# TensorE's order: from edges behind a planner to the program's own text, in a four-branch decoder step

## The chip, the cores and the metric

One core of a Trainium2 chip. The metric is the device time of one execution in microseconds; the median of the runs counts. A core has TensorE (PE in the profile; its weight loads are shown apart as PEld), VectorE (DVE), ScalarE (ACT), GpSimd (POOL) and SyncE (SP), which issues most DMAs. Each engine works through its own instruction queue in order, and waits there for semaphores.

## The reference

One inference step of a two-layer decoder trunk, d_model 1024, for 1024 prompt tokens and 64 sample tokens (8 sequences of 8) with shared weights. Everything is float32.

```
layer 0 (even): proj = rmsnorm(x) @ w_in_even
  branch A: y_a = a_b * short_conv(a_c * a_h) * silu(a_z)
  branch B: r, k, v, w, a from the token-shifted projection
            S = S*decay + (S @ -kk)*(kk*a) + v*k ;  y = S @ r      # a scan over time, 8 heads x 64
            y_b = (groupnorm(y) + bonus) * silu(b_z)
  x += concat(y_a, y_b) @ w_out_even
layer 1 (odd): proj = rmsnorm(x) @ w_in_odd
  branch C: y_c = (causal window means of 2, 4, 8, 16 - p) @ pool_w * scale * silu(c_z)
  branch D: y_d = u * (tril(W) @ layernorm(v) + b) * silu(d_z)
  x += concat(y_c, y_d) @ w_out_odd
y = rmsnorm(x)
```

The final states (convolution, shift, S, pooling) are outputs too.

## The kernel before

The activations lie transposed, features on partitions, tokens along the free axis. The 1088 tokens (64 sample, 1024 prompt) are cut into three blocks b0, b1, b2 of 320, 384 and 384 (`BLK`); b0 holds the sample and two groups of 128 prompt tokens, the others three groups each.

**Dense work.** A projection is a sequence of weight tiles of 128 output columns. `product` computes one tile for one block: for each of eight k-tiles three matmuls (lines 162, 163, 164) of split operands, hi x hi, hi x lo, lo x hi, so 24 matmuls into one PSUM tile ("dn"). Four k-tiles, 12 matmuls, are a half product; `marks` keeps the last instruction of each half. `weight` (from line 138) loads a raw tile in two pieces over SP's queue, casts it on ScalarE (whi, line 145) and subtracts on VectorE (wlo, line 146); each has `WB` = 4 buffers, two to a product. Layer 0 has 33 input tiles per block (13 shifted ones, 4 for the gate b_z, 16 for branch A in `mixer_a`) and 8 output tiles; layer 1 has 20 and 8.

**Branch B** is made of small matmuls. `rwkv_prep` prepares a group: decays and norms (lines 487, 488, 496), key transposes (521), score matrices of two chunks of 64 tokens (555, 64 matmuls), the bonus (577) and value transposes (584). `rwkv_inverse` inverts all triangular score blocks of a block on VectorE, 31 dependent pairs of operations (610, 612), between DMAs to and from DRAM on POOL's queue. `rwkv_merge` joins the halves of an inverse (639, 651). `rwkv_chunk` is the recurrence over chunks, each chunk's state SV coming from the chunk before (761, 770 and 775; then 780; then 786 and 788). `group_norm` and `group_out` (732) finish a group and store it to DRAM (`yr`), from where `out_proj0` loads it. `rwkv_sample` does the eight sample sequences (825, 846, 847, 858, 864, 883); at 858 it needs block 0's inverse. The PSUM tiles "pp" (4 buffers) serve all of these.

**What sets the order.** The program runs under a planner that orders every engine's instructions by priorities and by its own estimate of when inputs are ready; `tc.high_priority()` (also called `urgent`) puts a part ahead. TensorE's dense matmuls are chained by `later()`, an edge that says "not before the last product", and the branch's generators are walked in `recur`, each step with an edge "not before the half product `marks[x]`". These edges only say what a matmul comes after; what it comes before is the planner's choice, one matmul at a time.

**Order of the program.** b0: input tiles, preparation and inverse, `mixer_a`; b1: input tiles, `mixer_a`, then traced behind it, with the priority of `boost`, the recurrence of b0, the sample, and the preparation and inverse of b1; b2 likewise with the recurrence of b1; then output tiles of b0 and b1 with the recurrence of b2; output tiles of b2; layer 1. In layer 1 `pool_in(g)` makes six products, `windows` sums them on VectorE, and `pool_out` (line 1230) multiplies the sums; `layer_norm` (1146, 1166) works on ten token tiles.

Of the kernel before, what the change touches and what calls it, by code (L numbers as in the profile page):

```python
# [18 lines left out]
AT = (10, 10, 0)  # L19
EARLY, RATE, PREP_RATE = 20, 0.7, 0.5  # L20
# [53 lines left out]
def build(nc, tc, a):  # L74
    from contextlib import ExitStack
    ctx = ExitStack()

# [72 lines left out]
    order, marks = {}, []  # L150

    def later():

        return tc.issue_after(order["last"]) if order else ExitStack()

    def product(ps, w, h, c0, n):

        with later():
            for k in range(KT):
                wh, wl = w[k // 4]  # L160
                hh, hl = h[k]
                mm(ps, wh[:, k % 4, :], hh[:, c0:c0 + n], start=k == 0, stop=False)  # L162
                mm(ps, wh[:, k % 4, :], hl[:, c0:c0 + n], start=False, stop=False)  # L163
                i = mm(ps, wl[:, k % 4, :], hh[:, c0:c0 + n], start=False, stop=k == KT - 1)  # L164
                if k in (3, 7):
                    marks.append(getattr(i, "ins", i))
        order["last"] = marks[-1]
# [114 lines left out]
    def rms_token(B):  # L282
        B.ms0 = mk(ev, [128, 4], "rms_m", 2)
        with later():
            token_rstd(B.acc, B.n, B.ms0, pd, "dn")

    def rms_spread(B):
        with later():
            B.rstd = spread_rstd(B.ms0, B.n, ev, pd, "dn")
# [451 lines left out]
    def rwkv_chunk(B, g, c, parts, yps):  # L741
# [23 lines left out]
        first = state.get("y")  # L765
        for e in range(2):
            for p in range(4):
                if p == 0:
                    with (tc.issue_after(first) if first is not None else ExitStack()):
                        i = mm(yps[half[e], cols(p, 256 * c)], AR[half[e], p, c, 1, :], SV[half[e], p, e, :],  # L770
                               start=True, stop=False, skip_group_check=True)
                    first = getattr(i, "ins", i)
        with tc.issue_after(first):
            for p, e in heads[2:]:
                mm(yps[half[e], cols(p, 256 * c)], AR[half[e], p, c, 1, :], SV[half[e], p, e, :],
                   start=False, stop=False, skip_group_check=True)
# [10 lines left out]
        for p, e in heads:  # L787
            i = mm(yps[half[e], cols(p, 256 * c)], GT[:, 2 * p + e, 64:128], UV[:, p, e, :], start=False, stop=True,
                   skip_group_check=True)
        state["y"] = getattr(i, "ins", i)  # L790
# [14 lines left out]
    def rwkv_sample(B, now):  # L805
# [45 lines left out]
        up = pp()  # L851
# [75 lines left out]
    def late_rstd(psp, pname, pb=2):  # L927

        while late:
            B, acc = late.pop()  # L930
            B.ms = mk(cpool, [128, 4], f"ms1_{B.i}")
            with later(), urgent():
                token_rstd(acc, B.n, B.ms, psp, pname, pb)
# [12 lines left out]
    def recur(B, at, nxt=None):  # L946


        done, merged, now = [0], [0], [0]
        start = at  # L950
# [8 lines left out]
        def chain():  # L959
# [3 lines left out]
            for g in range(B.ng):  # L963
# [14 lines left out]
                done[0] += 1  # L978
# [5 lines left out]
        def prep():  # L984
            for q, x in enumerate(nxt.gl):
                while done[0] < min(q + 1, B.ng):
                    yield
                yield from rwkv_prep(nxt, *x)
                yield

        streams = [[at, RATE, merge()], [at, RATE, chain()]]
        if B.i == 0:
            streams.append([at - EARLY, RATE, rwkv_sample(B, now)])
        if nxt is not None:
            rwkv_begin(nxt)
            streams.append([at, PREP_RATE, prep()])
        while streams:
            x = min(streams, key=lambda x: x[0])
            now[0] = x[0] >= start
            with (tc.issue_after(marks[int(x[0])]) if x[0] < len(marks) else ExitStack()):  # L1000
                if next(x[2], 0) is not None:
                    streams.remove(x)
            x[0] += x[1]
        for p in range(4):
            ydr[(B.i, 4 + p)] = B.yr[:, p, :]

    def boost(mark):
        return tc.high_priority(tc.cur_priority - mark)
# [12 lines left out]
    mark = tc.cur_priority  # L1021
# [4 lines left out]
    rms_spread(b1)  # L1026
    mixer_a(b0, hs[0], (3,))
    hs.append(rms_h(b1))
    at = len(marks)
# [11 lines left out]
    at = len(marks)  # L1041
    rwkv_in(b2)
    mixer_a(b2, hs[2], range(4))
    with boost(mark):
        recur(b1, at + AT[1], b2)
        rwkv_inverse(b2)
    at = len(marks)
    out_proj0(b0)
    out_proj0(b1)
    with boost(mark):  # L1050
        recur(b2, at + AT[2])
# [73 lines left out]
    with later(), urgent():  # L1125
        norm1(b2)
# [4 lines left out]
    with tc.issue_after(order["last"]):  # L1131
        mm(ps, ones, ws.rearrange("p g t -> p (g t)"), start=True, stop=True)
# [3 lines left out]
    with tc.issue_after(order["last"]):  # L1136
        mm(ps[:, 0:256], ones[0:64], wss.rearrange("p g t -> p (g t)"), start=True, stop=True)
# [32 lines left out]
    def layer_norm(at):  # L1170
        last = None
        for ti in range(10):
            with tc.issue_after(marks[at + ti]):
                nx = ln_a(ti) if ti < 9 else None
            if last:
                with tc.issue_after(marks[at + ti + 1]):
                    ln_b(*last)
            last = nx
# [45 lines left out]
    def pool_out(g, cz, pl_):  # L1224
        yc = big()
        y1.append(yc)
        for B in Bs:
            ps = mk(pl, [128, 512], "pl", None)[:, :B.n]
            with later():
# [4 lines left out]
    at, last = len(marks), None  # L1234
    for g in range(4):
        cz, ep, es = pool_in(g)
        if g == 0:
            with urgent():
                layer_norm(at)
# [41 lines left out]
    def final_token(B):  # L1281
        B.msf = mk(e1p, [128, 4], "rms_m", 2)
        with later():
            token_rstd(accs[B.i], B.n, B.msf, pl, "pl", PLB)

    def final(B):
        with later():
            r = spread_rstd(B.msf, B.n, hp, pl, "pl", "rx", pb=PLB)
# [92 lines left out]
```

## Time and profile before

| | |
|---|---|
| median of 3 runs | 1141.25 us (1135.46 to 1141.45) |
| the profiled execution: time, span | 1138.0 us, 1136.2 us |
| mean granted TensorE clock | 0.967 |
| TensorE busy, weight loads busy | 1090.4 us (96%), 1003.7 us (88%) |
| VectorE busy | 729.5 us (64%) |
| ScalarE, GpSimd busy | 491.5 us (43%), 164.4 us (14%) |

The span goes from the first to the last instruction. TensorE's busy time is the union of its matmuls' times, whose ends are modelled, so a busy TensorE need not be one that works at its best. [...]

### The profile page before, as it was taken

How to read it: one execution, taken by the hardware profiler on the slowest of the kernel's cores; microseconds unless marked ns; L12 is line 12 of the kernel's file. 1: busy time of each engine (PE TensorE's matmuls, PEld its weight loads, DVE VectorE, ACT ScalarE, POOL GpSimd, SP SyncE). 2: the span in 40 equal slices, each digit the busy share in tenths (PEclk: the TensorE clock that was granted, in tenths of full speed). 3: DMA queues.
4: the chain of work that ended last, by engine and by line, in shares of the span. 5: the costliest groups of instructions: out<-in, count | busy, mean ns of one | idle time of the engine just before them, and what ended most of it. 6: DMA issues, size and time to landing. Idle time of an engine off the chain costs nothing.

```text
span 1136.2 us, 22856 instructions
## 1 busy us (share of the span) xinstructions
PE 1090.4 (96%) x8719; PEld 1003.7 (88%) x8719; DVE 729.5 (64%) x1526; ACT 491.5 (43%) x1017; POOL 164.4 (14%) x282
## 2 busy tenths in 40 slices
PE   7999999999999999999899999999999999999996
PEld 6998999876756899878799889899999999999995
DVE  7878899457632799478797477695373442245456
ACT  6376654365412554666535654464212111133232
POOL 2313343110301212113301011001010100000000
PEclk9999999899966999999999999899999999999998
DMA  8464563554412454535545687775201111112455
GB/s 263 149 212 129 157 206 123 146 157 145 128 58 65 121 189 125 140 104 150 155 152 149 185 242 222 228 254 186 79 21 55 38 48 38 53 41 91 116 154 183
DMA packets 135341, 154.91 MB, mean 136 GB/s; under 512 B 45560, under 2 KB 88696, under 8 KB 135232
## 3 DMA queue, kind: packets, MB, share of 16 engines
q1 hardware_dynamic: 130912, 146.36, 41.8%
q0 software_dynamic: 2256, 5.03, 2.2%
q10 hardware_dynamic: 2064, 2.08, 0.6%
q8 instruction: 68, 1.11, 0.4%
q14 instruction: 41, 0.34, 0.1%
HBM read 127.77 MB, written 25.64 MB: 135 GB/s over the span
## 4 chain that ended last, share of the span: by engine, by line
PE 40%; DVE 5%; DMA 4%; issue 1%; ACT 1%; POOL 1%; SPq 0%; DVEq 0%; ACTq 0%; POOLq 0%
PE dn L162 12%; PE dn L163 12%; PE dn L164 12%; DMA xn<-xd 2%; DVE wlo L146 1%; PE pl L1166 1%; DVE lo L171 1%; PE pl L1230 1%; DMA wraw<-wout 1%; DVE xn L1071 1%; POOL gvs L712 0%; DMA ma<-yd 0%; ACT whi L145 0%; DMA ma<-yr 0%; PE pp L732 0%
## 5 line engine op out<-in xcount | busy, mean ns | idle before, releaser
L162 PE MATMUL dn<-hi,whi 128*128 128x384 f32 (+1 forms) x1648 | 557.4, 338 | 12.9 <-ACT whi L145 6.5
L163 PE MATMUL dn<-lo,whi 128*128 128x384 f32 (+1 forms) x1648 | 551.9, 335 | 0.4 <-DVE lo L171 0.2
L164 PE MATMUL dn<-hi,wlo 128*128 128x384 f32 (+1 forms) x1648 | 551.5, 335 | 0.3 <-DVE wlo L146 0.3
L145 ACT CAST whi<-wraw 128x512 fp32r<-128x512 f32 x326 | 201.0, 619 | 347.1 <-PE dn L163 287.9
L162 PEld LDWEIGHTS dn<-hi,whi 128*128 128x128 f32 x1648 | 314.5, 191 | 25.2 <-ACT whi L145 6.9
L146 DVE TENSOR_TENSOR wlo<-wraw,whi 128x512 fp32r<-128x512 f32 x326 | 223.4, 687 | 159.5 <-ACT whi L145 146.8
L164 PEld LDWEIGHTS dn<-hi,wlo 128*128 128x128 f32 x1648 | 314.4, 191 | 8.5 <-issue 5.6
L163 PEld LDWEIGHTS dn<-lo,whi 128*128 128x128 f32 x1648 | 314.9, 191 | 7.7 <-issue 3.7
L183 POOL TENSOR_TENSOR rms_m<-rms_m,nhalf 128x3 f32<-128x3 f32 (+2 forms) x8 | 6.9, 870 | 218.3 <-DVE rms_m L182 218.3
L555 PE MATMUL pp<-AR,BK 64*64 64x128 f32 x544 | 36.3, 289 | 1.9 <-DVE BK L538 1.6
L555 PEld LDWEIGHTS pp<-AR,BK 64*64 64x64 f32 x544 | 22.0, 138 | 13.9 <-issue 9.8
L612 DVE TENSOR_TENSOR iv<-iv,prod 80x31 f32<-80x31 f32 (+23 forms) x93 | 31.3, 336 | 2.0
L610 DVE TENSOR_TENSOR prod<-iv 80x31 f32<-80x31 f32 (+23 forms) x93 | 31.2, 336 | 1.8
L565 POOL DMA_DIRECT2D dl<-GT x32 | 20.3, 636 | 77.8 <-DVE GT L558 77.8
L712 POOL TENSOR_TENSOR gvs<-gvs,nhalf 128x8 f32<-128x8 f32 (+1 forms) x9 | 15.1, 1674 | 113.0 <-DVE gvs L711 100.6
L1272 DVE TENSOR_TENSOR big<-dn,x1s 128x384 f32<-128x384 f32 (+1 forms) x24 | 12.8, 534 | 27.7 <-PE dn L164 27.7
L558 DVE TENSOR_TENSOR GT<-pp,cst 128x512 f32<-128x512 f32 x34 | 22.1, 683 | 12.3 <-PE pp L555 12.3
L324 POOL COPY q<-carry 128x1 f32<-128x1 f32 x26 | 22.5, 866 | 48.5 <-DVE KS L339 19.7
L1278 ACT ACTIVATE sq<-big 128x384 f32<-128x384 f32 (+1 forms) x21 | 10.7, 508 | 35.1 <-DVE big L1272 35.0
L796 DVE TENSOR_TENSOR pch<-pch,SV 64x256 f32<-64x256 f32 x32 | 13.9, 434 | 17.9 <-PE pch L786 16.3
L500 POOL TENSOR_TENSOR rn<-rn,nhalf 128x8 f32<-128x8 f32 (+1 forms) x9 | 15.5, 1719 | 48.7 <-DVE rn L499 48.7
L326 DVE TENSOR_TENSOR d<-q 128x384 f32<-128x384 f32 (+1 forms) x39 | 20.6, 529 | 1.9 <-ACT q L320 1.5
(279 smaller groups left out, 1246.9 us busy)
## 6 DMA issues: line engine op xcount, KB each, us to landing
wraw<-win SPq DMA_DIRECT2D x246, 256.0 KB, 2.8
wraw<-wout SPq DMA_DIRECT2D x80, 256.0 KB, 3.0
x<-xT SPq DMA_DIRECT2D x48, 192.0 KB, 3.7
xd<-x SPq DMA_DIRECT2D x16, 192.0 KB, 3.1
xn<-xd SPq DMA_DIRECT2D x16, 192.0 KB, 3.9
x1s<-xd SPq DMA_DIRECT2D x16, 192.0 KB, 2.4
yT<-big SPq DMA_DIRECT2D x16, 192.0 KB, 3.7
i<-vd SPq DMA_DIRECT2D x34, 64.0 KB, 2.6
```

The source lines that it names most:

```text
L145: A.copy(hi, raw)
L146: tt(lo, raw, hi.bitcast(F32), ALU.subtract)
L162: mm(ps, wh[:, k % 4, :], hh[:, c0:c0 + n], start=k == 0, stop=False)
L163: mm(ps, wh[:, k % 4, :], hl[:, c0:c0 + n], start=False, stop=False)
L164: i = mm(ps, wl[:, k % 4, :], hh[:, c0:c0 + n], start=False, stop=k == KT - 1)
L324: G.tensor_copy(q[:, 0:1], carry[:, j:j + 1])
L326: tt(d[:, :n], q[:, 0:n], q[:, 1:1 + n], ALU.subtract)
L555: mm(gp[e][o:o + 64, p * 128:(p + 1) * 128], BK[b:b + 64, p, c, q ^ (e if g is not None else 0), :], AR[b:b + 64, p, c, :, :].rearrange("p ...
L558: tt(GT[:, e::2, :], v3(gp[e]), m[e].unsqueeze(1).broadcast_to([128, 4, 128]), ALU.mult)
L565: nc.gpsimd.dma_start(of_half(B.dl[i], e), GT[64 * e:64 * e + 64, e::2, 0:64])
L610: tt(pr, X[:Q, 0:k, q:q + 1].broadcast_to([Q, k, r]), Lb[:Q, q:q + 1, k:32].broadcast_to([Q, k, r]), ALU.mult)
L612: tt(o, o, pr, ALU.add)
```

## The change

TensorE is taken out of the planner (`manual_schedule` for PE alone): its instructions now stand in the order in which the program writes them. The other engines are planned as before. `later`, `marks`, `issue_after` on matmuls and the constants `AT`, `EARLY`, `RATE`, `PREP_RATE` go. In their place the generators are registered by `weave(gen, after, rate)`, and `product` calls `half_done()` after each half product, which walks every stream whose position has come: one step of a generator, up to its next `yield`, is put out whole and at high priority, and the stream's position grows by its rate. The sums of squares for b0, the preparation of b0 with its inverse, the sample, the recurrences, the preparation of b1 and b2 and the layer norm become such streams. Preparation starts 27 half products after its block's beginning with two steps a half; recurrences start 4, 8 and 4 halves into the next part with one step a half (0.9 halves a step in the last). `finish()` puts out what is left before the output tiles of b2. Steps of `rwkv_prep`, `rwkv_merge`, `rwkv_chunk` and `group_out` are unchanged.

```diff
+    ctx.enter_context(tc.manual_schedule(engines={mybir.EngineType.PE}))
...
+    streams, halves = [], [0]
+    def weave(gen, after=0, rate=1.0):
+        streams.append([halves[0] + after, rate, gen])
+    def step(x):
+        with tc.high_priority():
+            if next(x[2], 0) is not None:
+                streams.remove(x)
+        x[0] += x[1]
+    def half_done():
+        halves[0] += 1
+        while streams and (x := min(streams, key=lambda x: x[0]))[0] <= halves[0]:
+            step(x)
+    def finish():
+        while streams:
+            step(min(streams, key=lambda x: x[0]))
     def product(ps, w, h, c0, n):
-        with later():
-            for k in range(KT):
+        for k in range(KT):
...
-                    marks.append(getattr(i, "ins", i))
-        order["last"] = marks[-1]
+                half_done()
...
+        def rstd():
             token_rstd(acc, n, B.ms0, pc, "pp", 4)
+            yield
             spread_rstd(B.ms0, n, ev, pc, "pp", "d", XTs[2].rearrange("p a b -> p (a b)"), 4)
...
+        weave(rstd(), 1)
...
-        while not now[0]:
-            yield
         for _ in rwkv_merge(B, None):
             yield
+        up = pp()
...
+    def prep(B, before=None):
+        rwkv_begin(B)
+        for q, x in enumerate(B.gl):
+            while before is not None and before.done < min(q + 1, before.ng):
                 yield
+            yield from rwkv_prep(B, *x)
+            yield
+        rwkv_inverse(B)
...
     hs.append(raw_h(b0))
+    weave(prep(b0), 27, 0.5)
     rwkv_in(b0)
-    rwkv_begin(b0)
-    for x in b0.gl:
-        with urgent() if x[2] is not None else ExitStack():
-            for _ in rwkv_prep(b0, *x):
-                pass
-    rwkv_inverse(b0)
     rms_stat(b1)
     mixer_a(b0, hs[0], (0,))
     rms_token(b1)
     mixer_a(b0, hs[0], (1, 2))
     rms_spread(b1)
+    weave(rwkv_sample(b0), 2)
     mixer_a(b0, hs[0], (3,))
     hs.append(rms_h(b1))
+    for x in recur(b0):
+        weave(x, 4)
+    weave(prep(b1, b0), 27, 0.5)
     rwkv_in(b1)
...
-    with boost(mark):
-        recur(b0, at + AT[0], b1)
-        rwkv_inverse(b1)
     hs.append(rms_h(b2))
+    for x in recur(b1):
+        weave(x, 8)
+    weave(prep(b2, b1), 27, 0.5)
     rwkv_in(b2)
     mixer_a(b2, hs[2], range(4))
+    for x in recur(b2):
+        weave(x, 4, 0.9)
     out_proj0(b0)
     out_proj0(b1)
+    finish()
...
-            with later():
-                mm(ps, pw[:, g, :], pl_[:, B.c0:B.c0 + B.n], start=True, stop=True)
+            mm(ps, pw[:, g, :], pl_[:, B.c0:B.c0 + B.n], start=True, stop=True)
...
+    weave(layer_norm(), 1)
     for g in range(4):
         cz, ep, es = pool_in(g)
-        if g == 0:
-            with urgent():
-                layer_norm(at)
         if last:
             pool_out(*last)
         last = g, cz, windows(g, ep, es)
```

## Rows read from the trace of the kernel before

**Rows 1.** The page, part 1: each engine's busy us, share, instructions.
```profile
PE 1090.4 (96%) x8719; PEld 1003.7 (88%) x8719; DVE 729.5 (64%) x1526; ACT 491.5 (43%) x1017; POOL 164.4 (14%) x282
```

**Rows 2.** TensorE in order of time, layer 1: start, us, line, out<-in, form.
```profile
959.66 0.34 PE L163 MATMUL dn<-lo,whi 128*128 128x384 f32 x1
...
963.83 0.33 PE L163 MATMUL dn<-lo,whi 128*128 128x384 f32 x1
```

**Rows 3.** Stretch 275.5 to 400 (tile whi's, all engines' busy us), line 912's range.
```profile
275.50:400.00 124.50, 70.90 (x204) 0.82 0.33 97
275.50:400.00 124.50, 121.81 (x650) 89.65 (x647) 62.78 (x122) 43.23 (x86) 21.96 (x33) 0.82 0.33 97
L912 DVE TENSOR_TENSOR x<-dn,x x24: 481/553/558, 628.3 to 764.4; 128x384 f32<-128x384 f32 x16, 128x320 f32<-128x320 f32 x8
```

**Rows 4.** TensorE in order of time at 278 us.
```profile
278.35 0.33 PE L786 MATMUL pch<-i 128*64 128x64 f32 x2
278.61 0.44 PE L162 MATMUL dn<-hi,whi 128*128 128x384 f32 x1
278.98 0.33 PE L786 MATMUL pch<-i 128*64 128x64 f32 x2
279.23 0.44 PE L163 MATMUL dn<-lo,whi 128*128 128x384 f32 x1
```

**Rows 5.** TensorE in order of time at 648 to 657 us, around three steps.
```profile
648.30 0.31 PE L164 MATMUL dn<-hi,wlo 128*128 128x320 f32 x1
...
649.95 0.69 PE L761 MATMUL pch<-SV,GT 128*64 128x64 f32 x16 [0.71 <-PE pp L692]
...
651.53 0.42 PE L162 MATMUL dn<-hi,whi 128*128 128x320 f32 x1
...
653.25 0.31 PE L164 MATMUL dn<-hi,wlo 128*128 128x320 f32 x1
...
654.10 0.42 PE L162 MATMUL dn<-hi,whi 128*128 128x320 f32 x1
...
655.82 0.31 PE L164 MATMUL dn<-hi,wlo 128*128 128x320 f32 x1
...
657.14 0.41 PE L162 MATMUL dn<-hi,whi 128*128 128x320 f32 x1
```

**Rows 6.** TensorE in order of time at 286 and at 557 us.
```profile
285.87 1.98 PE L555 MATMUL pp<-AR,BK 64*64 64x128 f32 x64
...
556.89 1.13 PE L577 MATMUL pp<-tm,cst 128*128 128x512 f32 x2 [0.23 <-DVE GT L558]
...
558.51 0.42 PE L164 MATMUL dn<-hi,wlo 128*128 128x384 f32 x1
```

**Rows 7.** TensorE and VectorE in order of time at the program's start.
```profile
6.48 0.64 PE L162 MATMUL dn<-hi,whi 128*128 128x320 f32 x1 [6.48 <-ACT whi L145]
...
9.78 0.47 PE L164 MATMUL dn<-hi,wlo 128*128 128x320 f32 x1
...
14.65 0.49 DVE L253 TENSOR_TENSOR acc<-acc,tm 128x320 f32<-128x320 f32 x1
...
15.29 0.78 PE L179 MATMUL pp<-onesc,acc 128*128 128x1 f32 x6
```

**Rows 8.** VectorE's busy us in 56 to 157.8; the inverse's lines, first and last.
```profile
56.00:157.80 101.80, 87.65 (x192) 1.00 0.59 177
...
L610 DVE TENSOR_TENSOR prod<-iv x93: 181/355/422, 157.8 to 606.1; 96x31 f32<-96x31 f32 x4, 96x60 f32<-96x60 f32 x4, 96x87 f32<-96x87 f32 x4, 96x112 f32<-96x112 f32 x4
L614 POOL DMA_DIRECT2D dl<-iv x6: 932/1274/1584, 198.9 to 608.3; - x6
```

**Rows 9.** DMAs on the tile dl (scores, inverses), from issue to landing.
```profile
DMA to landing us min/median/max: 2.0/2.9/8.2
```

**Rows 10.** DMAs on the tile yr: stores of group outputs, time to landing.
```profile
L739 SPq DMA_DIRECT2D yr<-iP x9: 543/561/563, 247.1 to 706.7; - x9
DMA to landing us min/median/max: 2.3/3.2/4.5
```

**Rows 11.** TensorE and VectorE in order of time at 928 to 938 us.
```profile
927.94 1.99 PE L1230 MATMUL pl<-big,pw 128*128 128x320 f32 x6
...
937.44 0.18 DVE L1219 TENSOR_TENSOR big<-t,ep 128x16 f32<-128x16 f32 x1
```

More of the change, by code (lines that the diff above doesn't have):

```diff
@@ L148, in weight @@
         return out
-    order, marks = {}, []
-    def later():
-        return tc.issue_after(order["last"]) if order else ExitStack()
-    def product(ps, w, h, c0, n):
-        with later():
-            for k in range(KT):
[L160 to L165, printed above, removed]
-                    marks.append(getattr(i, "ins", i))
-        order["last"] = marks[-1]
+    streams, halves = [], [0]
[13 more added lines that the diff above has]
+            step(min(streams, key=lambda x: x[0]))
+    def product(ps, w, h, c0, n):
+        for k in range(KT):
+            wh, wl = w[k // 4]
+            hh, hl = h[k]
+            mm(ps, wh[:, k % 4, :], hh[:, c0:c0 + n], start=k == 0, stop=False)
+            mm(ps, wh[:, k % 4, :], hl[:, c0:c0 + n], start=False, stop=False)
+            mm(ps, wl[:, k % 4, :], hh[:, c0:c0 + n], start=False, stop=k == KT - 1)
+            if k in (3, 7):
+                half_done()
     def split_to(hi, lo, x):
@@ L283, in rms_token @@
         B.ms0 = mk(ev, [128, 4], "rms_m", 2)
-        with later():
-            token_rstd(B.acc, B.n, B.ms0, pd, "dn")
+        token_rstd(B.acc, B.n, B.ms0, pd, "dn")
     def rms_spread(B):
-        with later():
-            B.rstd = spread_rstd(B.ms0, B.n, ev, pd, "dn")
+        B.rstd = spread_rstd(B.ms0, B.n, ev, pd, "dn")
     def rms_h(B):
@@ L763, in rwkv_chunk @@
         A.copy(RH, v3(rps[:, 0:256]))
[L765 to L776, printed above, removed]
+        for p, e in heads:
+            mm(yps[half[e], cols(p, 256 * c)], AR[half[e], p, c, 1, :], SV[half[e], p, e, :],
+               start=p == 0, stop=False, skip_group_check=True)
         yield
@@ L787, in rwkv_chunk @@
         for p, e in heads:
-            i = mm(yps[half[e], cols(p, 256 * c)], GT[:, 2 * p + e, 64:128], UV[:, p, e, :], start=False, stop=True,
-                   skip_group_check=True)
-        state["y"] = getattr(i, "ins", i)
+            mm(yps[half[e], cols(p, 256 * c)], GT[:, 2 * p + e, 64:128], UV[:, p, e, :], start=False, stop=True,
+               skip_group_check=True)
         yield
@@ L803, in rwkv_chunk, with rwkv_sample @@
         state["SV"] = SVn
-    def rwkv_sample(B, now):
+    def rwkv_sample(B):
         GT, AR = B.GT[4], B.AR[None]
@@ L931, in late_rstd @@
             B.ms = mk(cpool, [128, 4], f"ms1_{B.i}")
-            with later(), urgent():
+            with urgent():
                 token_rstd(acc, B.n, B.ms, psp, pname, pb)
@@ L944, in rwkv_in, with recur @@
         in_proj_bz(B, hs[B.i])
-    def recur(B, at, nxt=None):
-        done, merged, now = [0], [0], [0]
-        start = at
+    def recur(B):
+        merged = [0]
+        B.done = 0
         def merge():
@@ L977, in chain @@
                 last = group_norm(yps, 128), B.gl[g + B.i0][0], 128
-                done[0] += 1
+                B.done += 1
                 yield
@@ L982, in chain @@
             group_out(B, *last)
[L984 to L988, printed above, removed]
-                yield
[L991 to L1008, printed above, removed]
+            for p in range(4):
+                ydr[(B.i, 4 + p)] = B.yr[:, p, :]
+        return merge(), chain()
+    def prep(B, before=None):
+        rwkv_begin(B)
+        for q, x in enumerate(B.gl):
+            while before is not None and before.done < min(q + 1, before.ng):
+                yield
+            yield from rwkv_prep(B, *x)
+            yield
+        rwkv_inverse(B)
     b0, b1, b2 = Bs
@@ L1124, in build @@
     v_in((0,), (b1,))
-    with later(), urgent():
+    with urgent():
         norm1(b2)
@@ L1130, in build @@
     ps = mk(pl, [128, 512], "pl", None)
-    with tc.issue_after(order["last"]):
-        mm(ps, ones, ws.rearrange("p g t -> p (g t)"), start=True, stop=True)
+    mm(ps, ones, ws.rearrange("p g t -> p (g t)"), start=True, stop=True)
     for g in range(4):
@@ L1135, in build @@
     ps = mk(pl, [128, 512], "pl", None)
-    with tc.issue_after(order["last"]):
-        mm(ps[:, 0:256], ones[0:64], wss.rearrange("p g t -> p (g t)"), start=True, stop=True)
+    mm(ps[:, 0:256], ones[0:64], wss.rearrange("p g t -> p (g t)"), start=True, stop=True)
     for g in range(4):
@@ L1168, in ln_b, with layer_norm @@
             stt(MX[g][:, c0:c0 + T], mp[:, g * T:(g + 1) * T], P("ln_g", g), c[:, g, :], ALU.mult, ALU.add)
-    def layer_norm(at):
+    def layer_norm():
         last = None
         for ti in range(10):
-            with tc.issue_after(marks[at + ti]):
-                nx = ln_a(ti) if ti < 9 else None
+            nx = ln_a(ti) if ti < 9 else None
+            yield
             if last:
-                with tc.issue_after(marks[at + ti + 1]):
-                    ln_b(*last)
+                ln_b(*last)
             last = nx
@@ L1228, in pool_out @@
             ps = mk(pl, [128, 512], "pl", None)[:, :B.n]
-            with later():
-                mm(ps, pw[:, g, :], pl_[:, B.c0:B.c0 + B.n], start=True, stop=True)
+            mm(ps, pw[:, g, :], pl_[:, B.c0:B.c0 + B.n], start=True, stop=True)
             s = slice(B.c0, B.c0 + B.n)
             stt(yc[:, s], ps, P("pscale", g), cz[:, s], ALU.mult, ALU.mult)
-    at, last = len(marks), None
+    last = None
+    weave(layer_norm(), 1)
     for g in range(4):
         cz, ep, es = pool_in(g)
-        if g == 0:
-            with urgent():
-                layer_norm(at)
         if last:
@@ L1282, in final_token @@
         B.msf = mk(e1p, [128, 4], "rms_m", 2)
-        with later():
-            token_rstd(accs[B.i], B.n, B.msf, pl, "pl", PLB)
+        token_rstd(accs[B.i], B.n, B.msf, pl, "pl", PLB)
     def final(B):
-        with later():
-            r = spread_rstd(B.msf, B.n, hp, pl, "pl", "rx", pb=PLB)
+        r = spread_rstd(B.msf, B.n, hp, pl, "pl", "rx", pb=PLB)
         s = slice(B.c0, B.c0 + B.n)
```

12 lines of the change are left out of this document (removed).

## The prediction

> **What bounds the kernel now.** I read the page first, then stretches, then TensorE's order in time. TensorE is busy 96% of the span [rows 1], so only time on TensorE counts. How much of it is the dense work? In an undisturbed part of layer 1 (the odd layer) 24 matmuls of 384 columns take 963.83 - 959.66 = 4.17 us [rows 2], 0.174 us each; for 320 columns I scale to 0.145. A weight tile for the three blocks is 24 x (2 x 0.174 + 0.145) = 11.8 us. Layer 0 (even) has 41 tiles, 485 us; layer 1 has 28, 331 us. Layer 0 runs from 6.5 us to the last evacuation of its output projection at 764.4 [rows 3], which follows its product by about 2: some 756 us. So 271 us of layer 0 are not dense work: about 3,500 small matmuls of preparation, recurrence and sample, and waits. Layer 1 has 374 - 331 = 43 us of such time. The change can only win in the 271.
>
> The reader should then see what form that time has. In 275.5 to 400 the tile whi is read by 204 matmuls; two of three dense ones read it, so 306 ran, 53 us at 0.174, in 124.5 us, at a granted clock of 0.82 [rows 3]. [...] At 656 us 32 small ones put out together cost 657.14 - 655.82 - 0.145 = 1.17 us, 0.07 for two [rows 5]. [...]
>
> **The change part by part.**
>
> *Steps put out whole.* Prices come from the places where they are whole already. Recurrence, per chunk: first step 651.53 - 648.30 - 0.145 = 3.08 us, of which 0.71 a wait; second 654.10 - 653.25 - 0.145 = 0.70; third 1.17 [rows 5]. Together 4.2 to 4.95, for 16 chunks 68 to 79 us. Merges (two steps of 32 at 0.7) and output transposes (32 at 1.2), eight groups: 21 more. I take 95. Preparation of a group: 64 matmuls L555 1.98 us, L577 with L584 558.51 - 556.89 = 1.62 [rows 6], and some 28 others that I put at 2.5 by these rows (an estimate, 2 to 3): 6.2; eight groups and the shorter sample 54. Sample about 15 and row sums 6, estimates at the same prices. Sum 170 (160 to 180) against 271: 101 us to win, if nothing waits.
>
> *Waits that the text's order puts in.* TensorE now stands at each step until its inputs are there, with all dense work queued behind it.
> (a) The first sum of squares (L179) came at 15.29, after 41 dense matmuls; now it comes after 12, at 9.9 us, while its last input (L253) is written from 14.65 to 15.1 [rows 7]: 5 us.
> (b) First block. The sample's step that reads block 0's inverse (L858) falls in the text at half product 69: it is woven two halves after half 58, one step a half, tenth step. TensorE's own work to there is 6.5 + 66 x 1.74 + 3 x 2.1 + 23 of small work (three preparations 16, sums 2, sample 5) = 151 us. VectorE must have done all of the block's work and the inverse before it. Before, half 69 stood at about 157.8 us, just where the inverse's first operation starts [rows 8], with VectorE idle for 102 - 88 = 14 us since 56. The inverse is 31 pairs of operations, 62 x 0.34 = 21 us. So VectorE is through at 157.8 + 21 - 14 = 165 if it uses all that idle time and at 179 if none; (a) moves this and TensorE's own 151 alike by 5. TensorE waits 14 to 28 us; I take 20, since preparation is a chain that leaves VectorE gaps.
> (c) Preparation in blocks 1 and 2: from its first matmuls to L555 there are four halves (8.3 us), while sum, power, copy, transposes and eight VectorE operations must pass. Below 0, above 3.5 for each of six groups: 9. Four PSUM buffers shared with the recurrence: 4.
> (d) Inverses of blocks 1 and 2 have 30 and 26 halves (62 and 54 us) from the end of preparation to the merge's first matmuls (L639); block 0's operations alone were spread over 157.8 to 198.9 [rows 8], 41 us, and two DMA hops follow. The merge's loads on SP are put out one step, 2.1 us, ahead of L639 and take 2.0 to 8.2 to land [rows 9]; preparation's stores stay on POOL's queue. 0 to 20, I take 8.
> (e) Third block's recurrence: its chain starts at 5.8 halves and has 30 more steps at 0.9, so the last falls at 32.8, after the 32 halves of the two output projections, and is put out by finish(). Its result takes 1.3 us of transposes, 2.7 of ScalarE and VectorE, a DMA out and one in of 2.3 to 4.5 each [rows 10] and 1.1 for the split, about 11.6, with half a product (2.1) ready beside it; the last tile, for which a buffer comes free only then, 1.5 more. Before, the last store was issued at 706.7 [rows 10], under dense work. I take 11.
> (f) Left-over gaps between blocks, and the clock after long waits: 10.
> Sum 67 (30 to 110).
>
> *Layer 1.* pool_out(3) stands in the text right behind the last product of pool_in(3). The window sums that it reads end at 937.44 + 0.18 (L1219), while pool_out(2) began at 927.94 on TensorE and took 1.99 [rows 11]; two dense products lay between. They now queue behind it. VectorE loses 0.5 us of other work in that chain, so TensorE idles 937.1 - 929.9 = 7.2 us. The layer norm's steps, alternating before, save 3; clock 2. Net 6 lost.
>
> [...]
>
> *Sum.* The profiled execution took 1138.0 us (span 1136.2), 0.3% under the median of 1141.25. 1138 - 101 + 67 + 6 = 1110.
>
> **The rivals.**
> *Waits stay small.* VectorE fills its gaps (b at 9), preparation and inverses arrive in time (c, d near 0): waits 35, time 1078. For it: outside the first block VectorE is busy for half of 275.5 to 400, 62.78 of 124.5 us [rows 3]. Against: (a), (e) and pool_out are read off the text and can't vanish.
> *The gain becomes waiting.* Steps are whole, the clock stays up, but waits add to about 95: 1138. It needs (c) and (d) near their upper ends.
> *Slower: the inverse starves the weights.* In the trace its operations stand between weight splits (L146) and evacuations. Now it is put out as one high-priority step: 21 us back to back. [...] It decides once VectorE leaves the weights alone for over 17 us in each block. Against: weights are high priority too.
> *The change doesn't do what it says*, small matmuls whole but no cheaper: rows 5 and 6 exclude it; no chance of its own.
>
> **How the numbers follow.** Forecast 1110 (1094 to 1132): 0.50. Small waits: 0.16. Gain lost in waits: 0.15. Starved: 0.19. A measurement tells about 0.5% from no change, here 1135.5 to 1147.0. Faster 0.68 (the first two and 0.02 of the third), same 0.13, slower 0.19. The range 1077 to 1150 takes in the forecast, the third case, half of the small waits and a third of the starved case: 0.8.
>
> **What would show it.** Right: no alternation; 275 to 400 at a clock near 1.0; the merge and chunk steps at the prices above; a wait of some 5 us at L179, a long one at block 0's inverse, some 8 us at the last output projection of layer 0 and at pool_out(3). Wrong, if TensorE's idle time in layer 0 stays under 35 us or passes 95, if the inverse's operations run unbroken while TensorE idles, or if the small matmuls in whole steps cost more than in rows 5.

## The result and the profile after

The changed kernel takes 1220.6 us (median of 4 runs, 1214.7 to 1225.4) beside 1141.4 for the kernel before (4 runs on the same chip): a ratio of 1.070, 95% interval 1.063 to 1.077. It is slower; the forecast of 1110 and the whole range to 1150 missed it.

The page of the changed kernel, its first part, answers to [rows 1]:

```profile
PE 1069.0 (88%) x8719; PEld 1007.2 (83%) x8719; DVE 737.3 (61%) x1526; ACT 492.2 (40%) x1017; POOL 155.4 (13%) x282
```

TensorE works 21 us less than before and idles 148 us (1217.0 - 1069.0) in place of 46. To see where, both spans are divided at the same four dense matmuls: the first of b1, of b2, of the output tiles of b0, and of layer 1. A row gives the stretch, its length, busy us of TensorE, its weight loads, VectorE, ScalarE and GpSimd, then the granted clock (1.00 is full speed), DMA share and GB/s. The kernel before:

```profile
0.00:150.50 150.50, 139.78 (x1067) 133.48 (x1068) 124.94 (x278) 90.21 (x179) 44.82 (x99) 1.00 0.60 182
150.50:413.80 263.30, 255.26 (x1866) 207.18 (x1866) 164.48 (x346) 114.24 (x245) 50.10 (x69) 0.90 0.43 127
413.80:620.10 206.30, 198.50 (x2048) 184.38 (x2047) 162.41 (x355) 110.31 (x230) 44.18 (x69) 0.98 0.50 147
620.10:762.20 142.10, 135.21 (x1557) 125.75 (x1556) 97.02 (x192) 79.92 (x172) 7.62 (x9) 0.98 0.72 221
762.20:1136.20 374.00, 361.66 (x2189) 352.87 (x2187) 180.67 (x359) 96.80 (x192) 17.66 (x37) 0.99 0.28 87
```

The changed kernel:

```profile
0.00:183.10 183.10, 152.00 (x1107) 145.65 (x1108) 137.20 (x311) 95.25 (x195) 44.45 (x100) 0.94 0.53 161
183.10:426.80 243.70, 203.52 (x1827) 183.29 (x1826) 168.61 (x346) 110.03 (x229) 40.83 (x67) 0.92 0.46 132
426.80:643.40 216.60, 195.68 (x2048) 183.27 (x2047) 148.05 (x314) 109.87 (x231) 40.23 (x66) 0.95 0.46 135
643.40:804.80 161.40, 139.20 (x1555) 128.33 (x1555) 100.00 (x201) 80.66 (x173) 10.98 (x11) 0.90 0.66 197
804.80:1217.00 412.20, 378.58 (x2190) 366.63 (x2188) 183.44 (x358) 96.40 (x192) 18.91 (x38) 0.95 0.25 79
```

Only b1's stretch became shorter, by 19.6 us: there the alternation of dense and small matmuls of [rows 3, 4] is gone (some 40 of its small matmuls moved to b0's stretch; the other rows hold the same matmuls in both kernels, but for one or two at the edges). The others lost 32.6, 10.3, 19.3 and, in layer 1, 38.2. Over layer 0 (the first four rows) TensorE's busy time falls by 38.4 us, 728.8 to 690.4, and its idle time rises by 80.9, from 33.5 to 114.4.

What TensorE waited for, in the changed kernel (tile, line, the releaser's engine, tile and line; us in total, times, longest):

```profile
PE pp L860 <- DMA xt<-dl: 20.8, 1, 20.8
PE pp L653 <- DMA x<-dn: 18.3, 4, 10.5
PE pp L535 <- ACT tm L532: 15.6, 5, 6.9
PE pl L1147 <- DVE big L1149: 14.2, 27, 1.8
PE pp L569 <- DVE BK L552: 11.6, 6, 4.5
PE dn L176 <- ACT hi L183: 8.7, 2, 8.4
PE pl L1209 <- DVE big L1199: 7.5, 1, 7.5
PE dn L176 <- ACT yst L381: 7.1, 3, 4.6
...
PE pp L885 <- DVE tm L883: 6.3, 3, 3.8
PE pp L192 <- DVE acc L266: 5.0, 1, 5.0
```

Lines moved: 858 is 860, 639 is 653, 521 is 535, 555 is 569, 1166 and 1230 are 1147 and 1209, 610 is 624. No single wait makes the loss: inverses (L860, L653) and their users, preparation (L535, L569), the layer norm (L1147), pool_out(3) (L1209), the edge of the last output projection (hi L183), evictions (yst).

Here a wait costs more than its length. TensorE in order of time, around the longest:

```profile
214.76 1.94 PE L860 MATMUL pp<-tm,xt 64*64 64x64 f32 x16 [20.79 <-DMA xt<-dl]
216.63 0.69 PE L176 MATMUL dn<-hi,whi 128*128 128x384 f32 x1
...
220.77 0.94 PE L866 MATMUL pp<-GT,i 128*64 128x64 f32 x16
```

The twelve dense matmuls behind the wait take 220.77 - 216.63 = 4.1 us, where [rows 2] give 2.1. The granted clock over them is 0.50, where it was 1.00 just ahead of the wait (190.0 to 193.9 us). It is 0.50 too over 3 us behind a wait of 6.92 us that ends at 92 us, and 1.00 ahead of that one (84.0 to 85.1 us):

```profile
216.60:220.70 4.10, 4.10 (x13) 3.70 (x12) 0.00 (x0) 0.68 (x2) 0.00 (x0) 0.50 0.58 135
92.00:95.00 3.00, 2.94 (x12) 2.95 (x13) 1.79 (x5) 1.96 (x6) 0.00 (x0) 0.50 0.16 57
```

### The profile page after: what moved, and what is told of

Read it like the earlier page. It is cut to its first block, busy times and chain, and to the rows that moved or that the text cites. A ratio compares the mean times of both kernels' runs of the same rounds, so it can differ in the third digit from the quotient of the medians.

```text
span 1217.0 us, 22814 instructions
## 1 busy us (share of the span) xinstructions
PE 1069.0 (88%) x8719; PEld 1007.2 (83%) x8719; DVE 737.3 (61%) x1526; ACT 492.2 (40%) x1017; POOL 155.4 (13%) x282
## 4 chain that ended last, share of the span: by engine, by line
PE 39%; DVE 7%; DMA 2%; issue 1%; ACT 1%; POOL 1%; SPq 0%; DVEq 0%; ACTq 0%; POOLq 0%
PE dn L176 12%; PE dn L177 11%; PE dn L178 11%; DVE wlo L145 2%; PE pl L1147 1%; DVE big L1149 1%; DVE prod L624 1%; PE pl L1209 1%; DMA ma<-yr 1%; DMA xd<-x 1%; DVE iv L626 1%; PE pl L1127 0%; DVE wp L1189 0%; ACT whi L144 0%; DVE lo L184 0%
## 5 line engine op out<-in xcount | busy, mean ns | idle before, releaser
L176 PE MATMUL dn<-hi,whi 128*128 128x384 f32 (+1 forms) x1648 | 570.2, 346 | 27.5 <-ACT hi L183 8.7
L178 PE MATMUL dn<-hi,wlo 128*128 128x384 f32 (+1 forms) x1648 | 551.8, 335 | 0.0
L176 PEld LDWEIGHTS dn<-hi,whi 128*128 128x128 f32 x1648 | 321.0, 195 | 40.5 <-ACT hi L183 9.5
L177 PEld LDWEIGHTS dn<-lo,whi 128*128 128x128 f32 x1648 | 321.5, 195 | 5.5 <-DVE lo L184 3.4
L178 PEld LDWEIGHTS dn<-hi,wlo 128*128 128x128 f32 x1648 | 321.0, 195 | 0.2 <-DVE wlo L145 0.2
L569 PE MATMUL pp<-AR,BK 64*64 64x128 f32 x544 | 18.8, 287 | 11.6 <-DVE BK L552 11.6
L569 PEld LDWEIGHTS pp<-AR,BK 64*64 64x64 f32 x544 | 16.1, 142 | 14.8 <-issue 10.5
L914 DVE TENSOR_TENSOR x<-dn,x 128x384 f32<-128x384 f32 (+1 forms) x24 | 12.8, 532 | 25.7 <-PE dn L178 25.6
L1147 PE MATMUL pl<-ws,vh 128*128 128x128 f32 x64 | 15.6, 328 | 11.6 <-DVE big L1149 11.6
L1147 PEld LDWEIGHTS pl<-ws,vh 128*128 128x128 f32 x64 | 10.7, 200 | 16.4 <-DVE big L1149 16.4
L653 PE MATMUL pp<-x,GT 32*32 32x32 f32 x256 | 6.9, 204 | 18.3 <-DMA x<-dn 18.3
L1228 DVE TENSOR_TENSOR big<-big,dz 128x384 f32<-128x384 f32 (+1 forms) x12 | 6.4, 534 | 27.2 <-ACT dz L1227 27.2
```

Source lines behind the costliest of these rows:

```text
L569: mm(gp[e][o:o + 64, p * 128:(p + 1) * 128], BK[b:b + 64, p, c, q ^ (e if g is not None else 0), :], AR[b:b + 64, p, c, :, :].rearrange("p ...
L914: tt(x[:, :n], ps, x[:, :n], ALU.add)
L1147: mm(mp[:, g * T:(g + 1) * T], vh[:T, g * 128:(g + 1) * 128], rhs, start=True, stop=True)
```

## The experiments

All are edits of the changed kernel unless another is named; each was run once beside the kernel before (1138.7, 1143.6, 1146.1 and 1142.5 us in the four batches), and the best was then timed. The spans of the changed kernel's four runs go from 1212.9 to 1223.6 us, so a single run within some 6 us of 1217.0 shows no change. The table, worked out from the stretches of each trace, divides the spans at layer 1's first dense matmul. The sections below name only what is not in it.

| run | layer 0 us | TensorE busy | idle | clock | layer 1 us | span |
|---|---|---|---|---|---|---|
| before | 762.2 | 728.8 | 33.5 | 0.96 | 374.0 | 1136.2 |
| changed | 804.8 | 690.4 | 114.4 | 0.93 | 412.2 | 1217.0 |
| e1_ln4 | 804.2 | 690.0 | 114.2 | 0.93 | 383.0 | 1187.2 |
| e2_sample | 823.3 | 696.8 | 126.5 | 0.92 | 413.9 | 1237.2 |
| e3_sample_recur | 818.7 | 697.6 | 121.1 | 0.92 | 412.2 | 1230.9 |
| e4_pairs | 1091.9 | 947.4 | 144.5 | 0.80 | 413.1 | 1505.0 |
| e5_copy_first | 807.8 | 690.4 | 117.4 | 0.93 | 414.3 | 1222.1 |
| e6_prep_slow | 804.8 | 689.2 | 115.6 | 0.93 | 408.1 | 1212.9 |
| e6b_prep_slow_late | 808.0 | 693.0 | 115.0 | 0.92 | 413.0 | 1221.0 |
| e7_places | 800.9 | 694.2 | 106.6 | 0.94 | 371.6 | 1172.5 |
| e8_pace_b1 | 821.1 | 698.6 | 122.5 | 0.93 | 409.5 | 1230.6 |
| e9_plan_a | 807.5 | 701.9 | 105.6 | 0.93 | 371.1 | 1178.6 |
| e9_plan_b | 816.9 | 709.2 | 107.6 | 0.92 | 372.7 | 1189.6 |
| e10_no_split | 769.4 | 685.7 | 83.7 | 0.95 | 413.6 | 1183.0 |
| e10_before_no_split | 772.3 | 740.9 | 31.4 | 0.94 | 373.4 | 1145.7 |
| e11_places_timed | 805.6 | 693.8 | 111.8 | 0.93 | 371.8 | 1177.4 |

### The layer norm's four pairs

`ln_b` writes four matmuls into one PSUM tile, each followed in the text by its eviction.

```diff
             mm(mp[:, g * T:(g + 1) * T], vh[...], rhs, start=True, stop=True)
+        for g in range(4):
             c = cbs if T == 64 else cb
             stt(MX[g][:, c0:c0 + T], mp[...], P("ln_g", g), c[:, g, :], ALU.mult, ALU.add)
```

> Changed kernel, with one edit: in the layer norm's second part the four matmuls of a token tile are traced before the four evacuations that read their one PSUM tile, so that the matmuls of a step no longer wait for VectorE one by one. Theory W (the loss is TensorE standing at steps whose inputs come late): the 14.2 us of waits of line 1147 on VectorE go, and the low-clock spells between 870 and 936 with them; the span of 1217.0 falls by 20 to 30 us. Rival C (the low clock comes from the whole small steps themselves, not from waits): at most 14 us, the clock in that stretch stays near 0.8. Rival O (the loss lies in layer 0 alone): under 5 us.

Measured: 29.8 us less than the changed kernel's span. One step in the changed kernel:

```profile
872.15 0.63 PE L1147 MATMUL pl<-ws,vh 128*128 128x128 f32 x2
873.22 0.52 PE L1147 MATMUL pl<-ws,vh 128*128 128x128 f32 x2 [0.45 <-DVE big L1149]
874.19 0.49 PE L1147 MATMUL pl<-ws,vh 128*128 128x128 f32 x2 [0.45 <-DVE big L1149]
875.12 0.49 PE L1147 MATMUL pl<-ws,vh 128*128 128x128 f32 x2 [0.45 <-DVE big L1149]
875.44 0.60 PE L1127 MATMUL pl<-cst,big 128*128 128x128 f32 x4
```

The same step with the edit:

```profile
866.52 1.05 PE L1147 MATMUL pl<-ws,vh 128*128 128x128 f32 x8
867.41 0.60 PE L1127 MATMUL pl<-cst,big 128*128 128x128 f32 x4
```

Each matmul waits for the eviction of the one before it: 875.44 - 872.15 = 3.3 us a step where 0.9 do. The kernel before has the same pairs, but its planner lets dense matmuls in between. Over the sixteen half products among which these steps lie (846.3 to 923.7 us) the changed kernel idles 14.2 us and its clock is 0.85; the kernel before (804.5 to 853.2) idles 0.4 at 1.00. With the edit the same half products (846.3 to 894.0) idle 1.3, again at 1.00. So half of the 28.7 us between the two kernels is waits, half slower work behind them, and both go with the edit.

### What moves when a step moves

The sample's steps, which meet the wait of 20.8 us, start 22 half products on in place of 2; then the recurrence of b0 16 on in place of 4 as well.

```diff
-    weave(rwkv_sample(b0), 2)
+    weave(rwkv_sample(b0), 22)
...
-        weave(x, 4)        # recur(b0), second run only
+        weave(x, 16)
```

> Changed kernel, with the sample woven 22 halves after half 58 in place of 2, so that its step that reads block 0's inverse comes 20 half products later. Theory W with VectorE as the late one: the 20.8 us wait at line 860 goes, but the merge of block 0 (line 653, half product 71) now stands for the same inverse, some 15 to 20 us; the span stays within 8 us of 1217. Rival S (each wait is a cost of its own): 20 us less, no long wait at the first merge.

> As the kernel before it, and block 0's recurrence woven 16 halves into block 1 in place of 4. Theory W: nothing on TensorE needs block 0's inverse before it is there; both waits go, and the slow spell behind them; 20 to 32 us under 1217. Rival V (VectorE is behind by that time whatever TensorE does, and the dense work then waits for evacuations and weights instead): under 8 us, with waits of dense matmuls on VectorE of 12 us and more between 183 and 240.

None of the theories expected a slower kernel: 20 and 14 us over the changed one. In the first run theory W was right on the waits alone: L860 waits for nothing, but the next user of the inverse, the merge, waits:

```profile
215.29 0.31 PE L653 MATMUL pp<-x,GT 32*32 32x32 f32 x2 [24.04 <-DMA x<-dn]
```

In the second that wait is 5.0 us, but the samples, b0's recurrence and b1's preparation now lie in the same half products: L885 waits 14.0 us in place of 6.3, L569 21.4 in place of 11.6, and b1's first merge 12.1 in place of 6.4.

### The alternation, priced

The 272 calls of L569 are put out one by one, each behind one dense matmul (`dense_done` takes the next one from the generator).

```diff
             mm(ps, wh[:, k % 4, :], hh[:, c0:c0 + n], start=k == 0, stop=False)
+            dense_done()            # behind each of the three matmuls
...
                            AR[b:b + 64, p, c, :, :].rearrange("p a s -> p (a s)"), start=True, stop=True)
+                        yield "pair"
```

> Changed kernel, with the 16 score matmuls of each of 17 chunks (line 569) put out one by one between dense matmuls, in place of 16 together: 272 alternations, the way the kernel before had them in part. Price of alternation as read before: 0.62 us from dense to dense against 0.174 and about 0.06 for the same small matmul in a whole step, so 0.39 each, 106 us; less the 11.6 us wait of line 569, and more where the clock falls: 85 to 130 us over 1217. Rival F (alternation is free, the old slow stretch was slow for other reasons): within 15 us of 1217.

Measured: 288 us more, 257 of it busy time of layer 0: 0.94 us a call. In this order of time the alternation runs first at a granted clock of 1.00 (115.25 to 115.95 us), then at 0.50 (127.75 to 131.85):

```profile
115.25 0.41 PE L192 MATMUL dn<-hi,whi 128*128 128x320 f32 x1
115.59 0.43 PE L588 MATMUL pp<-AR,BK 64*64 64x128 f32 x2
115.95 0.63 PE L194 MATMUL dn<-lo,whi 128*128 128x320 f32 x1
...
128.93 0.63 PE L192 MATMUL dn<-hi,whi 128*128 128x320 f32 x1
129.50 0.69 PE L588 MATMUL pp<-AR,BK 64*64 64x128 f32 x2
130.11 0.63 PE L194 MATMUL dn<-lo,whi 128*128 128x320 f32 x1
```

From dense to dense 0.70 us, then 1.18. The expectation's 0.62 is that of [rows 4], also at a clock of 1.00 (278.35 to 279.86 us); there two small matmuls cost 0.62 - 0.17 = 0.45 us, in the whole step of [rows 5] 0.07. Most of the alternation ran at the second price (the clock of layer 0 falls to 0.80), and the time went up by over twice what was allowed. So alternation is dear, and whole steps do remove it.

### A small copy's place in ScalarE's queue

The wait of 6.92 us at L535 (it ends at 92.06 us) in ScalarE's and GpSimd's order of time, changed kernel:

```profile
87.27 1.28 ACT L527 ACT_TABLE_LOAD   x1 [1.62 <-DVE tm L523]
88.56 0.63 ACT L527 ACTIVATE Pp<-tm 128x512 f32<-128x512 f32 x1
89.10 0.61 ACT L529 ACTIVATE iP<-tm 128x512 f32<-128x512 f32 x1
89.73 1.28 ACT L381 ACT_TABLE_LOAD   x1
91.03 0.47 ACT L381 ACTIVATE yst<-yst 128x320 f32<-128x320 f32 x1
91.40 0.60 ACT L532 COPY tm<-rn 128x512 f32<-128x512 f32 x1
```

```profile
85.60 1.86 POOL L514 TENSOR_TENSOR rn<-rn,nhalf 128x8 f32<-128x8 f32 x1
```

The copy's input is ready at 87.46; it runs at 91.40.

```diff
+        x = tmp()
+        i = A.copy(v3(x[:T], 8), rna[:T].unsqueeze(2).broadcast_to([T, 8, 64]))
         V.tensor_tensor_scan(...)
...
+        with tc.issue_after(i):          # the same for the second exponential
             act(Pp[:, :, :, 1:], c4p, AF.Exp, scale=-0.5 * KAPPA)
```

> The small ScalarE copy that the prep's transposes (L535) read is put ahead of the two exponentials in ScalarE's queue, in all blocks; TensorE's order is unchanged. Theory Q (the wait is the copy's place in ScalarE's queue: in block 0 its input was ready at 87.46 us and it ran at 91.40, behind two table loads of 1.28 us and three other instructions): the 15.6 us of L535's waits fall to 4 to 8 us and the span falls by 8 to 15 us, to 1202 to 1209. Theory C (the chain of small work behind each step is itself longer than the dense work between two steps): what L535 no longer waits, L569 waits for BK (11.6 us grows to 18 or more), and the span stays within 4 us of 1217.

Measured: span 1222.1. L535's waits fall only to 12.2, the first from 6.92 to 4.47, and L569's rise from 11.6 to 18.8, since the exponentials now come later. Theory C, though its span is a microsecond outside C's 4: the step's inputs end at about the same time whichever comes first.

### Preparation with room

```diff
-    weave(prep(b0), 27, 0.5)
+    weave(prep(b0), 27, 1.0)
```

The second run adds `weave(rwkv_sample(b0), 30)` and `weave(x, 20)` for b0's recurrence.

> Block 0's preparation gives one step for each half product in place of two; nothing else changes. Theory L (a wait is local, each step needs more dense work ahead of it): the waits of block 0's L535 and L569 (6.9, 3.1, 3.1, 4.5, 1.1 us) fall to under 6 us in sum, nothing grows elsewhere, and the span falls by 20 to 30 us with the clock's share, to 1187 to 1197. Theory D (the waits only move on, since the chain preparation, inverse, sample, recurrence is longer than the dense work laid beside it): block 0's waits shrink as much, the inverse starts 5 to 15 us later than at 151 us, L860's wait grows from 20.8 to 30 to 45 us, and the span stays within 8 us of 1217.

> Block 0's preparation with one step for each half product, block 0's recurrence from 20 half products on in place of 4, the samples' steps 28 half products later. Theory L: both block 0's preparation waits and the wait for the inverse go, and the span falls by 30 to 45 us, to 1172 to 1187. Theory D: the waits come back where the same steps now crowd (L653 of blocks 0 and 1, L885, L569), and the span lies between 1210 and 1250, as in the two runs that moved the samples and the recurrence (1237 and 1231).

Theory D both times: 1212.9 and 1221.0. In the first run block 0's preparation waits fall from 18.7 to 8.4 us, but the inverse starts at 160.2 in place of 149.4, and the debt is paid at two places further on, 6.1 us and 3.7 more than before (D had expected at least 9 more at L860):

```profile
162.68 1.94 PE L829 MATMUL pp<-GT,tm 128*128 128x64 f32 x8 [6.13 <-DMA tm<-wkv]
...
213.63 1.94 PE L860 MATMUL pp<-tm,xt 64*64 64x64 f32 x16 [24.53 <-DMA xt<-dl]
```

In the second, which puts the samples and the recurrence off, the dense work runs some 80 us ahead of the changed kernel's by the 83rd half product. It keeps nothing of it: b1's first merge waits 18.3 us and stands at 453.4 us, where the changed kernel has it at 452.0.

### Layer 1 mended, merges later

`e1_ln4`, pool_out(3) behind the next three dense products, `weave(x, 11)` for b1's recurrence, `weave(x, 9, 0.75)` for b2's:

```diff
-        if g == 0:
-            pool_out(*last)
...
         dense1(a["win1"][16 + g], h1, evz)
+        if g == 0:
+            pool_out(*last)
```

> Four matmuls ahead of four evictions in the layer norm (which gave 29.8 us alone), pool_out(3) behind the next three dense products in place of ahead of them, block 1's recurrence from 11 half products on in place of 8, block 2's from 9 in place of 4 with a step each 0.75 half product in place of 0.9. Layer 1, both theories: 38 to 42 us less than the changed kernel's 412 (30 from the layer norm, 7.5 of wait and 2 to 4 of clock from pool_out). Layer 0, theory L: L653's waits of 6.4 and 10.5 us fall under 4 us in sum and layer 0 ends 12 to 20 us earlier; span 1157 to 1167. Theory D: the waits go on to the next step of the chain or to the end of out_proj0(b1) (8.4 us there grows), layer 0 ends within 6 us of before; span 1173 to 1181.

Layer 1 takes 371.6 us, 40.6 less than changed and 2.4 less than before; its 38 us are accounted for. Layer 0 is 3.9 shorter, and 0.8 longer when the same kernel is run again (`e11_places_timed`): theory D. L653's waits fall from 18.3 to 7.8, but L535's rise from 15.6 to 19.2 and L569's from 11.6 to 14.2.

Timed as the best version found:

> The kernel of the new places once more, timed against the kernel before. Its one run gave 1174.3 beside 1143.6 us, so theory T (layer 1 is mended, layer 0 keeps its waits) expects a ratio of 1.022 to 1.034, and nothing in it can come out faster than the kernel before.

1177.0 us (4 runs) beside 1142.5 (7 runs): ratio 1.029, interval 1.024 to 1.034. No version beat the kernel before.

### Steps closer together

From the end of b1's inverse to the start of b2's the changed kernel takes 167 us (440 to 607), the kernel before 117 (452.4 to 569.5). Theory S said that this chain sets layer 0.

```diff
-        weave(x, 8)                     # recur(b1)
-    weave(prep(b2, b1), 27, 0.5)
+        weave(x, 8, 0.8)
+    weave(prep(b2, b1), 27, 0.3)
```

> Block 1's recurrence with a step each 0.8 half product in place of 1, block 2's preparation with a step each 0.3 half product in place of 0.5, so that block 2's inverse stands about 7 half products (some 15 us of dense work) earlier in TensorE's order. Theory S (the chain of small steps sets layer 0: from the end of block 1's inverse to the start of block 2's it takes 167 us in the changed kernel, 117 us in the kernel before): block 2's inverse starts 8 to 18 us before 607.3 us, the wait of 10.5 us ahead of block 2's first merge goes, and the span falls by 8 to 15 us, to 1202 to 1209. Theory T (TensorE is full, and each step that comes sooner waits itself): the waits of L535, L569 and L785 in that stretch grow by what L653 saves, and the span stays within 4 us of 1217.

> Layer 1 as in the run with new places (layer norm and pool_out: 38 us less). Layer 0: dense work alone beside each inverse, and the steps of the chain closer together between the inverses: block 0's preparation 1 half product a step, its recurrence from 24 half products on at 0.8 a step, the samples 24 half products later, block 1's preparation from 29 at 0.45, its recurrence from 9 at 0.8, block 2's preparation at 0.3, its recurrence from 1 at 0.85. Theory S: the waits for the three inverses (20.8, 6.4, 10.5 us) and half of block 0's preparation waits go, layer 0 is 25 to 45 us shorter; span 1134 to 1154. Theory T: the steps wait where they now crowd, layer 0 is within 10 us of the changed kernel's; span 1169 to 1189.

> As the plan before it, with block 0's preparation at 0.75 half product a step, the samples 18 half products later than in the changed kernel, block 0's recurrence from 20 at 0.8, block 1's preparation from 27 at 0.45, its recurrence from 8 at 0.8. Theory S: some of block 0's preparation waits stay and a wait of 5 to 10 us for its inverse; 5 to 10 us over the other plan, 1140 to 1164. Theory T: 1169 to 1189.

Theory S falls. Theory T comes nearer, but `e8_pace_b1` is 13.6 us over the changed kernel where T allowed 4. In it b2's inverse starts at 621, later, not sooner: L535 in that stretch waits 4.1, 5.2 and 3.4 us where it had waited 2.8. Both plans leave layer 0 longer than the changed kernel's, by 2.7 and 12.1 us, and plan a still shows

```profile
455.80 0.31 PE L653 MATMUL pp<-x,GT 32*32 32x32 f32 x2 [17.62 <-DMA x<-dn]
```

### Whose queue makes the inputs late

VectorE subtracts out the low half of the first weight piece alone, and all dense products of layer 0 read that one; the kernel leaves out the other subtractions.

```diff
-                tt(lo, raw, hi.bitcast(F32), ALU.subtract)
+                if lo is not first.get("used"):        # layer 0: one low half for all tiles
+                    tt(lo, raw, hi.bitcast(F32), ALU.subtract)
...
```

> The changed kernel with the low half of layer 0's weights worked out once only: every dense product of layer 0 then reads that first low half, so the dense results are left wrong, and VectorE has some 259 subtractions of 0.69 us (178 us) less; TensorE's instructions and their order are the same. Theory Q (the steps' inputs are late because they stand in VectorE's queue behind the weight splits): TensorE's idle time in layer 0 (107 us) falls by 35 us or more and the span by 35 to 60 us, to 1157 to 1182. Theory L (they are late by the chain of dependent work itself, each link a TensorE, ScalarE, VectorE or DMA time, with an empty queue too): the span falls by under 15 us, to 1202 to 1217.

> The kernel before with the same left out. Both theories: TensorE waits for little there (46 us in all), so its time falls by under 15 us, to 1123 to 1138. If it fell as much as the changed kernel, the splits would be a burden on both orders and no part of the difference.

The changed kernel's layer 0 falls by 35.4 us with VectorE relieved of 142 us in it (553.9 to 411.7 busy); the kernel before does not fall at all, against the expectation of 1123 to 1138 (1147.5 beside a median of 1142.5, whose runs go from 1139 to 1149). The three inverses, by the stretches that hold their 31 products (VectorE's busy us in these alone), changed kernel and changed kernel without the splits:

```profile
149.40:204.20 54.80, 10.44 (x31) 0.94 0.52 159
387.50:440.10 52.60, 10.39 (x31) 0.97 0.51 159
607.30:646.10 38.80, 10.40 (x31) 1.00 0.51 161
```

```profile
146.80:185.40 38.60, 10.36 (x31) 1.00 0.59 174
371.40:403.50 32.10, 10.45 (x31) 1.00 0.47 143
575.50:603.20 27.70, 10.40 (x31) 1.00 0.53 161
```

They shorten by 16, 20 and 11 us. L860's wait falls from 20.8 to 8.5 and L653's from 18.3 to nothing; L535 (15.5 for 15.6) and L569 (10.2 for 11.6) stay. So theory Q holds for the waits at the inverses, theory L for those in the preparation; the fall of 34 us, 31 of it idle time of layer 0, lies just under Q's 35. This separates the two kinds of wait. By the second expectation's own test the splits, since the kernel before doesn't fall without them, are a part of the difference: both kernels carry them, but only the fixed order makes TensorE stand behind VectorE's queue, for 31 of the 81 us of idle time that layer 0 gained.

## Why the prediction was wrong

**Right.** The reading that TensorE sets the time, and that small matmuls cost less in whole steps than in alternation with dense ones. A stretch without alternation gained: b1's, by 19.6 us.

**The step that failed: "Waits that the text's order puts in".** For layer 0 it counted 57 us of waits, from places that were read off one by one. Measured, without the start of 6.9 us:

| term | predicted | measured | at |
|---|---|---|---|
| (a) first sum of squares | 5 | 5.0 | L192 |
| (b) b0's inverse | 20 | 20.8 | L860 |
| b0's preparation | none | 18.7 | L535, L569 |
| (c) preparation of b1, b2, PSUM | 13 | 8.5 | L535, L569 |
| (d) inverses of b1, b2 | 8 | 18.3 | L653 |
| (e) last output projection | 11 | 8.7 | L176 <- hi |
| evictions of input tiles | none | 10.8 | L176 <- yst |
| inside sample and recurrence | none | 14 | L885, L785, L706 |

These make 105 of the 107.5 us; 43 us stood in no term. The single prices look good, (b)'s partly by luck: it had TensorE at its step at 151 us and VectorE through with the inverse at 165 to 179, and measured are 194.0, where TensorE begins to wait, and 204; the other 10 us of the wait are the way of the inverse to L860 over DMA, which (b) left out. (b) weighed TensorE's own work in b0 against VectorE's up to the inverse and let every preparation step in between pass freely; the waits left out held back both sides. The deeper fault is that each wait was taken as an event of its own. They are one dependent chain (preparation, inverse, merge, recurrence, next preparation) laid between fixed amounts of dense work: eight other orders left TensorE idle in layer 0 for 106 to 127 us, whichever wait they removed; only with VectorE's queue relieved did it fall clearly below, to 84. So a part of the chain's length is VectorE's queue, where the inverses stand among the weight splits. Under the planner dense matmuls stood inside the chain's gaps, at the price of alternating; whole steps buy the alternation back and lose the cover (this last is argued, see below). The prediction's own mark for being wrong, idle time in layer 0 over 95 us, is what came.

**(f), the clock.** The clock's part of (f)'s 10 us and the 2 us of clock in layer 1 were the author's estimate; no run shows these terms. What the runs show in their place: behind the wait of 20.79 us twelve dense matmuls take 2.0 us more (4.1 for 2.1) at a clock of 0.50, and behind the wait of 6.91 us at the start 22 waits of over 1 us came in layer 0. TensorE's busy time there is 690.4 us, 35 over the 485 of dense work and the 170 of whole steps. The trace shows where most of it lies: thirteen half products of dense work, each in a stretch with a granted clock of 0.50 to 0.61, took 1.1 to 2.8 us longer than an undisturbed one, 21 us together, while the small matmuls together stayed within their 170. So the steps were priced rightly, and the clock was not. At the program's very start twelve dense matmuls take 3.6 us by [rows 7] in place of 1.74, and the profile gives a clock of 1.00 over them, as in the changed kernel (6.4 to 10.0 us, 7.0 to 10.0); what makes them slow is not shown.

**Layer 1.** The layer norm was to save 3 us and cost 28.7: wrong sign, because the four pairs in one tile were read as alternation with dense work, not as a chain in which TensorE now stands. pool_out(3) is right in kind, 7.5 us of wait for 7.2.

**Rivals.** "The gain becomes waiting" is nearest in its mechanism, but its 95 us of waits were too few and it had no clock. "Starved weights" ended on the right side, but its mechanism did not occur: the matmuls that read wlo (L178) waited nowhere, and the inverses' operations, some 21 us a block, lay spread over 39 to 55 us.

**Open.** That the planner's order hides nearly all of the chain, while every order by half products with the splits in place exposes over 100 us, is shown by the counts. That it does so by letting dense matmuls into the steps is not shown: it takes a run that lets them into chosen steps alone, and that hybrid wasn't tried.

## What to carry to other kernels

Before fixing an in-order engine's order by text, write down for each step not only its price on that engine but how late its inputs are by all other engines' work, and how much independent work stands ahead of it; here the sum over known waits was a lower bound, since a step that no longer waited handed its debt to the next one of the same chain. Where matmuls and evictions share a PSUM tile, put out all matmuls first: here the planner, which mixed in other work, hid the waiting of each on the other, and the fixed order showed it at full length (3.3 us a step in place of 0.9). Try a new order one region at a time: here b1's stretch won 19.6 us, and layer 1, with two edits, some 2.

## What was not expected of the hardware

In the alternating run the granted clock lay at 0.50, and fell to it, without any idle time of TensorE. Three stretches that follow each other:

```profile
115.95:131.85 15.90, 15.90 (x41) 7.73 (x40) 1.40 (x3) 0.62 (x1) 0.32 (x1) 0.50 0.06 18
131.85:140.00 8.15, 8.15 (x31) 5.24 (x31) 2.55 (x5) 2.37 (x3) 1.32 (x2) 0.71 0.16 48
140.00:150.00 10.00, 10.00 (x27) 4.81 (x27) 0.69 (x1) 0.62 (x1) 0.00 (x0) 0.50 0.08 26
```

TensorE is busy throughout, in the first and the last with a 128x128 and two 64x64 tiles in turn, and its clock there is 0.50; the stretch of [rows 3], 0.82 as a whole, holds both 1.00 (275 to 310 us) and 0.50 (325 to 350). Ahead of the first fall a wait of 3.11 us had ended at 114.92. Ahead of the second there was none: from 132.47 on nine dense matmuls stood in a row, the alternation then ran at 0.70 us a period from 136.4 to 139.9, and behind that, with no idle time since 114.92, the clock fell again. What in the alternation brings it down was not tested.
